# Two transformer blocks in f32: every operand tile is moved to a multiple of 256 bytes in SBUF

## The chip, the cores and the metric

The kernel runs on one core of one Trainium2 chip. The metric is the device time of one execution in microseconds, the median of several. Before the change it is 2309.09 us (three runs, 2305.04 to 2309.76).

## The reference

Two blocks follow each other on one sequence of 1024 tokens of width 1024, all in float32. Cut to what is computed:

```python
# first block
h = rms_norm(x, mix_norm_g);  proj = h @ w_in          # 1024 x 3080
fq, fk, fv, flog, dq, dk, dv = split(proj)
c = cumsum(log_sigmoid(flog + b_forget))               # 8 heads of 64, causal
fox = softmax(fq @ fk.T / 8 + c[t] - c[s]) @ fv
a = softmax(q1 @ k1.T / 8 + alibi) - lam * softmax(q2 @ k2.T / 8 + alibi)
diff = rms_norm(a @ dv) * 0.8                          # 4 heads, values of 128
x = x + concat(fox, diff) @ w_out
h = rms_norm(x);  x = x + (silu(h @ w_gate) * (h @ w_up)) @ w_down   # d_ff = 2816
x = rms_norm(x)
# second block
h = rmsnorm(x);  u, q, k, v = split(h @ w_in_2)        # 1024 x 2048
a = (mean of u over windows of 2, 4, 8, 16, less u) @ w_pool * pool_scale
b = neighbourhood attention of q, k, v on a 16 x 64 grid, with a bias
x = x + concat(a, b) @ w_out_2
h = rmsnorm(x);  x = x + square(relu(h @ w_up_2)) @ w_down_2         # d_ff = 4096
return rmsnorm(x)
```

## The kernel before

Tokens lie in tiles of 128 rows. Every factor of a large product is split into a high and a low half of type fp32r (`split`, L105 to L107: ScalarE copies the high half, VectorE or GpSimd subtracts it to get the low half), and a product is the sum of three matmuls (high by high, high by low, low by high), summed in PSUM in float32. Almost all of TensorE's work is such matmuls with a moving operand of 128 x 512 (7,756 of them) or about 128 x 256 (1,728 of 256 columns and 192 of 264), each with a stationary operand of 128 x 128. The lines are L155 (`proj_T`, queries and keys), L167 (`proj_tok`, values; the first weight piece has 2 x 4 x 264 columns because the forget gates are in it), L181 (`down`, output projection), L732 (`prod`, the first product of both feed-forward parts: gate and up in the first block, up in the second), L1204 (`ffn_deep`, the down products) and L1467 (`pool_mix`).

TensorE's order is written by hand: in the attention, pieces of projections are woven between the steps of the heads; in the feed-forward part the product of one unit follows the other. The instructions of the other engines are ordered by a scheduler from the program's order and the pools. Weights come by DMA from SyncE's queue into raw slots (`Weights.prefetch`, L52; two slots of 128 x 2112 float32, 8448 bytes per partition), and `get` (L67 to L80) splits them into `wh` and `wl` tiles of at least 128 x 1024, which go round a ring: two of each in pool `w1`, two of each in pool `w1b` (L355), then in `w1` alone. The other raw tiles (L667, L775, L1058) use the same slots.

SBUF is filled from two sides: pools on the left are laid from the lowest address up, pools with `side="right"` from the highest down, so a tile's address follows from the sizes of all the tiles before it on its side. In the kernel before, nearly every tile's size is a multiple of 256 bytes, but a few are not: `mhalf` and `lam` (4 bytes), the raw slots, the small `st` tiles, `wh` of 1056 columns, `lf`, the bias `b` of L491, and `psc`, `ws` and `edge` in `pool_mix`. The operand tiles come to lie as follows; each number is the start address modulo 256.

| operand | line | start modulo 256, moving / stationary | matmuls |
|---|---|---|---|
| gate, up and up products | L732 | 224 / 160 | 3192 |
| down products | L1204 | 224 / 224 | 2268 |
| projections, first block | L155 | 224 / 224 and 224 / 96 | 432 and 336 |
| projections, second block | L155 | 160 / 224 | 576 |
| output projections | L181 | 224 / 224, 224 / 160, 160 / 160 | 480, 240, 48 |
| pool mixer | L1467 | 192 / 0 | 24 |
| values, 256 columns | L167 | 224 / 160, 224 / 224, 96 / 224 | 960 in all |
| values, 264 columns | L167 | from 224 or 96 in steps of 32 / 224 | 192 |

A moving operand of 512 columns is 2048 bytes of a partition, one of 256 columns is 1024 bytes, a stationary one 512 bytes.

Of the kernel before, what the change touches and what calls it, by code (L numbers as in the profile page):

```python
# [9 lines left out]
F32 = mybir.dt.float32  # L10
F32R = mybir.dt.float32r
# [5 lines left out]
P = 128  # L17
NT = 8
# [18 lines left out]
class Weights:  # L37


    def __init__(self, k, raw_pool, depth):  # L40
        self.k, self.raw_pool, self.depth = k, raw_pool, depth
        self.todo, self.loaded = [], []
        self.pool_low = False
# [4 lines left out]
    def prefetch(self, depth=None):  # L48
        while self.todo and len(self.loaded) < (depth or self.depth):
            ap = self.todo.pop(0)  # L50
            n = ap.shape[-1]
            raw = self.raw_pool.tile([P, 2112], F32, tag="raw", name="raw")  # L52
            self.k.nc.sync.dma_start(raw[:, :n], ap)
            self.loaded.append((raw, n))

# [11 lines left out]
    def get(self):  # L67

        self.prefetch(1)
        raw, n = self.loaded.pop(0)  # L70
        out, m = [], n // 2
        for k in range(2):
            pool = self.slots.pop(0)
            self.slots.append(pool)
            h = pool.tile([P, max(m, 1024)], F32R, tag="wh", name="wh")
            l = pool.tile([P, max(m, 1024)], F32R, tag="wl", name="wl")
            self.k.split(h[:, :m], l[:, :m], raw[:, k * m:(k + 1) * m], self.pool_low)
            out.append((h[:, :m], l[:, :m]))
        self.prefetch()
        return out  # L80


class Kern:
    def __init__(self, tc, ctx, a):
        self.tc, self.nc, self.a = tc, tc.nc, a
        nc = self.nc
        self.const = ctx.enter_context(tc.tile_pool(name="const", bufs=1))
        self.raw = ctx.enter_context(tc.tile_pool(name="rawp", bufs=2))
        self.sm = ctx.enter_context(tc.tile_pool(name="small", bufs=8))
        self.ps = ctx.enter_context(tc.tile_pool(name="ps", bufs=4, space=PSUM))  # L90
        self.dram = ctx.enter_context(tc.tile_pool(name="scr", bufs=1, space=DRAM))
        self.ident = self.const.tile([P, P], F32, name="ident")
        make_identity(nc, self.ident)
        self.mhalf = self.const.tile([P, 1], F32, name="mhalf")
        nc.vector.memset(self.mhalf, -0.5)
        self.w = Weights(self, self.raw, 2)

# [234 lines left out]
    def block1_mix(self, enter_x):  # L332
        nc, tc, a = self.nc, self.tc, self.a
# [9 lines left out]
        at_ctx = tc.tile_pool(name="att", bufs=2)  # L343
        at = at_ctx.__enter__()
        cT = at.tile([P, NT, 8], F32, name="cT", bufs=1)
        lam = at.tile([P, 1], F32, name="lam", bufs=1)
        tri = at.tile([P, P], F32, name="tri", bufs=1)
        gd = at.tile([P, P], F32, name="gd", bufs=1)
        at2_ctx = tc.tile_pool(name="att2", bufs=2)
        with tc.tile_pool(name="act", bufs=1, side="right") as apool, \  # L350
                tc.tile_pool(name="w1", bufs=2, side="right") as wp, \
                tc.tile_pool(name="stage", bufs=2, side="right") as st:
            self.act_tiles(apool)
            with tc.tile_pool(name="w1b", bufs=2, side="right") as wpb:
                self.w.ring((wp, 2), (wpb, 2))  # L355
                self.w.depth, self.w.pool_low = 1, True
                norm, trans = self.norm_load(at, 0)
                self.w.pool_low = False
                for t in range(NT):
                    norm(t)  # L360
                    if t == 1:
                        w = self.w.get()
                self.w.depth, self.w.pool_low = 2, True
                lf = at.tile([P, NT, 8], F32, name="lf", bufs=1)
                for t in range(NT + LAG):
                    if t < NT:
                        trans(t)
                    if t == 5:
                        w1 = self.w.get()
                        self.w.pool_low = False  # L370
                    if t >= LAG:
                        self.proj_v(st, w, vd, 0, t - LAG, lf)
                nc.sync.dma_start(tri, a["tri"])
                nc.sync.dma_start(gd, a["gd"][0:1, :].partition_broadcast(P))
                nc.vector.tensor_scalar(gd, gd, 1.0 - LAM_INIT, None, ALU.mult)
                self.lambda_(at, lam)
                for t in range(NT):
                    self.proj_v(st, w1, vd, 1, t, lf)
                    if t == 1:
                        finish = self.forget(at, lf, cT, cd)  # L380
                    if t == 3:
                        w = self.w.get()
                for n in range(2):
                    for f, _ in self.proj_qk(st, qd, kd, n, w):
                        f()
                    w = None
                    if n == 0:
                        w = self.w.get()
                        finish()
            at2 = at2_ctx.__enter__()  # L390
            self.w.ring((wp, 2))
            fill, done = [], {("f", 0): 0, ("f", 1): 0}
            for kind, i in self.FILL:
                if (kind, i) == self.FILL[-1]:
                    fill.append((lambda: setattr(self.w, "depth", 1), 0.0))
                if kind == "v":
                    fill += self.proj_v_all(st, vd, i)
                else:
                    fill += self.proj_qk(st, qd, kd, i if kind == "f" else 4 + i)
                done[kind, i] = len(fill)  # L400
            fox = lambda i: self.fox_pair(at, at2, i, qd[i], kd[i], vd, cd, cT, tri, mxd[i], done["f", i])
            diff = lambda h: self.diff_head(at, at2, h, qd[4 + h], kd[4 + h], vd, gd, lam, mxd[4 + h], done["d", h])
            units = fox(0) + fox(1) + diff(0) + fox(2) + diff(1) + fox(3) + diff(2) + diff(3)
            steps = self.pipeline(units)
            cut = next(n for n, m in enumerate(steps) if m[2:] and m[2] == len(fill))
            self.weave(steps[:cut], fill, 0.0, -LEAD1)
# [74 lines left out]
    def forget(self, at, lfT, cT, cd):  # L481
# [3 lines left out]
        lf = mk("lf")  # L485
        for t in range(0, NT, 4):
# [1 line left out]
            for k in range(4):  # L488
                nc.tensor.transpose(pf[:8, k * P:(k + 1) * P], lfT[:, t + k, :], self.ident)
            nc.vector.tensor_copy(lf[:, t * P:(t + 4) * P], pf[:8, :])  # L490
        b = at.tile([8, 1], F32, tag="bf", name="bf", bufs=1)  # L491
        nc.sync.dma_start(b, a["b_forget"])
        z, u, t1, t2, t3 = mk("z"), mk("u"), mk("t1"), mk("t2"), mk("t3")
        nc.vector.tensor_scalar(z, lf, b, None, ALU.add)
# [170 lines left out]
        return units  # L665

    def mix_raw(self, mxd, c):  # L667
        m = self.raw.tile([P, 2112], F32, tag="raw", name="mixin")
        m = m[:, :2048].rearrange("p (k t) -> p k t", k=2)
        for kk in range(2):  # L670
            self.nc.sync.dma_start(m[:, kk, :], mxd[2 * c + kk])
        return m
# [100 lines left out]
        self.split(h[:, :, j * P:(j + 1) * P], l[:, :, j * P:(j + 1) * P], ps.rearrange("p (k t) -> p k t", t=P))  # L773

    def load_raw(self, src):  # L775
        t = self.raw.tile([P, 2112], F32, tag="raw", name="raw")[:, :src.shape[-1]]
        self.nc.sync.dma_start(t, src)
        return t

# [82 lines left out]
    def ffn(self, x, xd, mxd, wo, close_w, gi, n, gated, wts, wd, md, finish):  # L862


        nc, tc = self.nc, self.tc
# [3 lines left out]
        mixin = self.mix_raw(mxd, 3)  # L869
# [53 lines left out]
        for t in range(NT):  # L923
# [14 lines left out]
            k = t % 2  # L938
# [47 lines left out]
        wc = 4 * 512  # L986
# [10 lines left out]
        for i in range(G):  # L997
# [7 lines left out]
            b = self.one()  # L1005
# [49 lines left out]
                p2(i + L)  # L1055

            if i == G - 4:
                t = self.raw.tile([P, 2112], F32, tag="raw", name="raw")[:, :wc]  # L1058
                raws += [t, self.load_raw(wts[i + 2])]
                nc.sync.dma_start(t, wsrc(0, 2, wc))  # L1060
            elif i + 2 < G:
                raws.append(self.load_raw(wts[i + 2]))
# [338 lines left out]
    def pool_mix(self, at, st, mxd):  # L1401
# [3 lines left out]
        wh = at.tile([P, 512], F32R, name="wph", bufs=1)  # L1405
        wl = at.tile([P, 512], F32R, name="wpl", bufs=1)
        self.split(wh, wl, wf)
        psc = at.tile([P, 4], F32, name="psc", bufs=1)
        nc.sync.dma_start(psc, a["pscale"])
        rc = at.tile([P, 64], F32, name="rc", bufs=1)  # L1410
        nc.sync.dma_start(rc, a["rcount"].partition_broadcast(P))
# [18 lines left out]
        def sums(g, n):  # L1430

            u, gs, size = state[g]["u"], state[g], 2 << g
            if n == 0:
                gs["s"], gs["m"] = at.tile([P, 1040], F32, tag="ws", name="ws", bufs=1), 1039
                nc.vector.tensor_tensor(gs["s"][:, :1039], u[:, 0:1039], u[:, 1:1040], ALU.add)
                return
            s = gs["s"]
            if n <= g:
                step = 1 << n
                m = gs["m"] = gs["m"] - step  # L1440
                nc.vector.tensor_tensor(s[:, :m], s[:, 0:m], s[:, step:m + step], ALU.add)
                return
            off = 8 - size // 2
            edge = at.tile([P, 16], F32, tag="edge", name="edge")
            for k, t0 in ((0, 0), (1, S - 8)):
                ek, r_ = edge[:, k * 8:k * 8 + 8], rc[:, g * 16 + k * 8:g * 16 + k * 8 + 8]
                nc.vector.tensor_tensor(ek, s[:, off + t0:off + t0 + 8], r_, ALU.mult)
# [313 lines left out]
```

## Time and profile before

| | |
|---|---|
| median of three runs | 2309.09 us (2305.04 to 2309.76) |
| the profiled execution: its own time | 2302.17 us |
| its span, first to last instruction | 2300.5 us |
| TensorE (PE) busy | 2220.8 us, 97% |
| VectorE (DVE) busy | 1493.3 us, 65% |
| ScalarE (ACT) busy | 997.3 us, 43% |
| GpSimd (POOL) busy | 812.3 us, 35% |
| mean share of the DMA engines | 46.4% on SyncE's queue, 148 GB/s |
| granted TensorE clock, mean | 0.991 |

All rows come from the one profiled execution. A row of the timeline gives the start of a group of like instructions, the time from its first start to its last end, the engine, the line and the form, with x4 for four of them. The matmuls overlap in the record: one of 512 columns is shown as 390 ns long, but the next starts some 230 ns later. The time that a matmul costs in a stream is therefore the distance from one start to the next, here called the pitch. It is read by dividing the distance of two rows by the matmuls between them, or, within one row of n, by taking the recorded length of one (0.39 us) from the row and dividing by n - 1.

### The profile page before, as it was taken

The page shows a single profiled execution, that of the slowest core. Times are in us where ns is not written, and L with a number is a line of the kernel's source. Part 1 is how long each engine was busy: PE and PEld are TensorE (multiplying, and loading weights), DVE is VectorE, ACT ScalarE, POOL GpSimd, SP SyncE. Part 2 cuts the span into 40 slices and gives each one's busy share as a digit, 9 for nine tenths or more (in the row PEclk, how much of TensorE's full clock was granted, in tenths as well). Part 3 has the DMA queues.
Part 4 walks back from the last instruction along what each step waited for, and adds up shares of the span by engine and source line. Part 5 has one row for each costly group of instructions (what it writes and reads, how often), then busy time and mean ns, then how long its engine had stood idle before and what let it go on. Part 6 is the DMA issues. An engine that isn't in the chain of part 4 may idle for free.

```text
span 2300.5 us, 30691 instructions
## 1 busy us (share of the span) xinstructions
PE 2220.8 (97%) x11148; PEld 1870.5 (81%) x11148; DVE 1493.3 (65%) x2510; ACT 997.3 (43%) x1826; POOL 812.3 (35%) x742
## 2 busy tenths in 40 slices
PE   8999999989999999999999999999999999999998
PEld 8888898867788888878887888878778887878886
DVE  5356666677854545457889725687754444688888
ACT  5245555644433222223333536663454444434333
POOL 1055656563432323233235302110432222233335
PEclk9999999999999999999999999999999999999999
DMA  6487575651424333336311379884335444733202
GB/s 230 144 231 200 153 209 151 193 174 45 158 96 167 122 110 109 111 126 231 133 69 55 94 207 255 234 243 138 119 99 193 155 137 143 272 147 128 74 37 83
DMA packets 128615, 343.42 MB, mean 149 GB/s; under 512 B 12616, under 2 KB 49864, under 8 KB 113104
## 3 DMA queue, kind: packets, MB, share of 16 engines
q1 hardware_dynamic: 128320, 341.20, 46.4%
q8 instruction: 88, 1.44, 0.3%
q14 instruction: 63, 0.52, 0.1%
q10 hardware_dynamic: 144, 0.26, 0.0%
HBM read 254.35 MB, written 87.06 MB: 148 GB/s over the span
## 4 chain that ended last, share of the span: by engine, by line
PE 74%; DVE 13%; issue 4%; POOL 3%; ACT 3%; DMA 2%; SPq 0%; ACTq 0%; POOLq 0%; DVEq 0%
PE one L732 27%; PE one L1204 17%; PE one L155 12%; PE one L167 5%; PE one L181 4%; DVE o L107 4%; PE one L280 2%; PE one L571 1%; DVE x L187 1%; PE one L223 1%; DVE x L1209 1%; PE one L222 1%; PE one L633 1%; DVE wl L107 1%; DVE e L235 1%
## 5 line engine op out<-in xcount | busy, mean ns | idle before, releaser
L1204 PE MATMUL one<-o 128*128 128x512 f32 x2268 | 520.7, 391 | 11.8 <-DVE o L107 11.8
L1204 PEld LDWEIGHTS one<-o 128*128 128x128 f32 x2268 | 425.6, 188 | 105.9 <-DVE o L107 17.7
L732 PE MATMUL one<-o,wh 128*128 128x512 f32 x1216 | 309.9, 398 | 15.9 <-DVE u L1009 8.1
L107 DVE TENSOR_TENSOR wl<-raw,wh 128x512 fp32r<-128x512 f32 (+2 forms) x254 | 206.0, 825 | 143.8 <-ACT wh L106 141.0
L732 PEld LDWEIGHTS one<-o,wh 128*128 128x128 f32 x1216 | 230.3, 191 | 70.6 <-ACT o L106 7.0
L106 ACT ACTIVATE wh<-raw 128x512 fp32r<-128x512 f32 (+2 forms) x278 | 185.8, 699 | 86.4 <-POOL raw L721 53.1
L721 POOL TENSOR_TENSOR s<-raw 128x512 f32<-128x512 f32 x38 | 54.6, 1438 | 471.1 <-DMA raw<-in_wgu_dram 233.0
L732 PE MATMUL one<-o,wl 128*128 128x512 f32 x608 | 164.9, 393 | 0.0
L239 ACT ACTIVATE e<-e,st 128x768 f32<-128x768 f32 (+7 forms) x128 | 99.4, 776 | 134.1 <-DVE st L235 131.8
L1209 DVE TENSOR_TENSOR x<-x,one 128x512 f32<-128x512 f32 x184 | 121.9, 677 | 52.4 <-PE one L1204 52.3
L732 PEld LDWEIGHTS one<-o,wl 128*128 128x128 f32 x608 | 115.0, 189 | 24.9
L155 PE MATMUL one<-actH,wh 128*128 128x512 f32 x448 | 124.0, 398 | 0.2 <-DVE ptl L107 0.2
L155 PE MATMUL one<-actH,wl 128*128 128x512 f32 x448 | 123.6, 397 | 0.0
L155 PE MATMUL one<-actL,wh 128*128 128x512 f32 x448 | 123.6, 397 | 0.0
L1365 POOL TENSOR_SCALAR ne<-ne,st 128x384 f32<-128x384 f32 x64 | 39.5, 618 | 225.9 <-DVE st L241 207.5
L106 ACT ACTIVATE o<-tb 128x1024 fp32r<-128x1024 f32 (+1 forms) x42 | 42.8, 1031 | 165.4 <-DVE tb L721 165.3
L1029 DVE TENSOR_TENSOR u<-one,p 128x512 f32<-128x512 f32 x38 | 26.3, 691 | 135.5 <-PE one L732 135.4
L554 POOL TENSOR_SCALAR b<-negc,cT 128x640 f32<-128x640 f32 (+3 forms) x64 | 50.1, 784 | 153.5 <-DVE st L235 93.2
L721 POOL TENSOR_TENSOR raw<-raw 128x512 f32<-128x512 f32 x76 | 99.2, 1306 | 6.0
L834 ACT ACTIVATE f<-f 128x512 f32<-128x512 f32 x33 | 20.9, 632 | 181.0 <-DVE f L827 162.8
L187 DVE TENSOR_TENSOR x<-one,x 128x512 f32<-128x512 f32 x128 | 82.4, 681 | 25.8 <-PE one L181 25.4
L850 ACT ACTIVATE f<-f 128x512 f32<-128x512 f32 x48 | 30.4, 632 | 156.0 <-DVE f L827 131.3
(254 smaller groups left out, 4961.9 us busy)
## 6 DMA issues: line engine op xcount, KB each, us to landing
raw<-in_wgu_dram SPq DMA_DIRECT2D x22, 1024.0 KB, 5.2
raw<-in_wup_dram SPq DMA_DIRECT2D x16, 1024.0 KB, 5.3
mr<-f SPq DMA_DIRECT2D x64, 256.0 KB, 4.9
raw<-in_wdn_dram SPq DMA_DIRECT2D x14, 1024.0 KB, 5.0
wq<-in_wdn_dram SPq DMA_DIRECT2D x12, 1024.0 KB, 9.1
nbias<-in_nab_dram SPq DMA_DIRECT2D x32, 384.0 KB, 4.9
mq<-mr SPq DMA_DIRECT2D x12, 1024.0 KB, 6.3
raw<-in_wgu_dram SPq DMA_DIRECT2D x22, 512.0 KB, 4.0
```

The source lines that it names most:

```text
L106: self.nc.scalar.activation(h, src, AF.Copy)
L107: (self.nc.gpsimd if pool else self.nc.vector).tensor_tensor(l, src, f32(h), ALU.subtract)
L155: self.nc.tensor.matmul(ps, lhsT=w_[:, k, cols:cols + P], rhs=ac[:, 4 * j + k, half * 512:half * 512 + 512], start=(n == 0), stop=(n == 23))
L167: self.nc.tensor.matmul(ps, lhsT=ac[:, 4 * j + k, t * P:(t + 1) * P], rhs=w_[:, k, :], start=(n == 0), stop=(n == 23))
L181: nc.tensor.matmul(dst[h], lhsT=a_[:, kk, t * P:(t + 1) * P], rhs=w_[:, h * 512:(h + 1) * 512], start=(n < 2), stop=(n >= last))
L187: nc.vector.tensor_tensor(xs, p_, xs, ALU.add)
L239: nc.scalar.activation(e, e, AF.Exp, bias=mx, scale=-1.0, accum_out=sm)
L554: nc.gpsimd.tensor_scalar(b[:, :nk], nc_row[:, :nk], cT[:, qt, h:h + 1], 1.0, ALU.add, ALU.mult)
L721: (self.nc.gpsimd if pool else self.nc.vector).tensor_tensor(out, a, b, ALU.subtract)
L732: self.nc.tensor.matmul(ps, lhsT=l, rhs=r, start=(first and n == 0), stop=(n == total - 1), skip_group_check=True)
L1204: nc.tensor.matmul(ps, lhsT=l[:, sl], rhs=r[:, sb], start=(start and n == 0), stop=(n == total - 1), skip_group_check=True)
L1209: nc.vector.tensor_tensor(dst, dst, ps, op)
```

## The change

The first tiles on each side are pads (`padl`, `padr`), so that what follows begins at a multiple of 256 bytes; the sizes that were no such multiple are rounded up, or the tile is made a part of another. The raw slots shrink from 8448 to 8192 bytes. The first weight piece, with 2112 columns, no longer fits a raw slot and gets a tile of its own in a new pool `w1c`; the split weights of the first pieces go round eight slots over three pools in place of four over two.

```diff
@@ Weights.prefetch
-            raw = self.raw_pool.tile([P, 2112], F32, tag="raw", name="raw")
+            if n > 2048:
+                raw = self.wider.tile([P, n], F32, name="raw", bufs=1)
+            else:
+                raw = self.raw_pool.tile([P, 2048], F32, tag="raw", name="raw")
@@ Weights.get
-            h = pool.tile([P, max(m, 1024)], F32R, tag="wh", name="wh")
-            l = pool.tile([P, max(m, 1024)], F32R, tag="wl", name="wl")
+            h = pool.tile([P, max(-(-m // 64) * 64, 1024)], F32R, tag="wh", name="wh")
+            l = pool.tile([P, max(-(-m // 64) * 64, 1024)], F32R, tag="wl", name="wl")
@@ Kern.__init__
         self.const = ctx.enter_context(tc.tile_pool(name="const", bufs=1))
+        self.const.tile([P, 32], F32, name="padl")
+        padr = ctx.enter_context(tc.tile_pool(name="padr", bufs=1, side="right"))
+        padr.tile([P, 56], F32, name="padr")
...
-        self.mhalf = self.const.tile([P, 1], F32, name="mhalf")
+        self.cols = self.const.tile([P, 64], F32, name="cols")
+        self.mhalf, self.lam = self.cols[:, 0:1], self.cols[:, 1:2]
@@ block1_mix
-        lam = at.tile([P, 1], F32, name="lam", bufs=1)
+        lam = self.lam
...
-            with tc.tile_pool(name="w1b", bufs=2, side="right") as wpb:
-                self.w.ring((wp, 2), (wpb, 2))
+            with tc.tile_pool(name="w1b", bufs=2, side="right") as wpb, \
+                    tc.tile_pool(name="w1c", bufs=2, side="right", reuse_waits="tile") as wpc:
+                self.w.wider = wpc
+                self.w.slots = [wpc, wpc, wp, wp, wpc, wpc, wpb, wpb]
...
-                lf = at.tile([P, NT, 8], F32, name="lf", bufs=1)
+                lf = at.tile([P, P], F32, tag="dt2", name="lf", bufs=4)[:, :64].rearrange("p (t h) -> p t h", h=8)
@@ forget
-        b = at.tile([8, 1], F32, tag="bf", name="bf", bufs=1)
+        b = at.tile([8, 64], F32, tag="bf", name="bf", bufs=1)[:, :1]
@@ mix_raw, load_raw, ffn: raw tiles
-        m = self.raw.tile([P, 2112], F32, tag="raw", name="mixin")
+        m = self.raw.tile([P, 2048], F32, tag="raw", name="mixin")
...
@@ pool_mix
-        psc = at.tile([P, 4], F32, name="psc", bufs=1)
+        psc = at.tile([P, 64], F32, name="psc", bufs=1)[:, :4]
...
-                gs["s"], gs["m"] = at.tile([P, 1040], F32, tag="ws", name="ws", bufs=1), 1039
+                gs["s"], gs["m"] = at.tile([P, 1088], F32, tag="ws", name="ws", bufs=1), 1039
...
-            edge = at.tile([P, 16], F32, tag="edge", name="edge")
+            edge = at.tile([P, 24], F32, tag="edge", name="edge")[:, :16]
```

With the change, all 7,756 matmuls of 512 columns and all 1,728 of 256 have both operands at 0 modulo 256. The 192 matmuls of 264 columns have the stationary operand at 0 and the moving one at 0, 32, 64 or 96, because their columns still follow each other in steps of 1056 bytes.

TensorE's and GpSimd's instructions keep their order. On the other three engines the order differs in the first 95 us alone. ScalarE, while the activations are normed and transposed (`actH` is an evacuated transposition, `vt` a finished value tile, `raw_405` and `raw_407` the third and fourth weight pieces), before:

```order
L106 ACTIVATE vt_378<-one_353 128x2x2x64
L106 ACTIVATE actH_123<-one_390 128x4x128
L106 ACTIVATE actH_123<-one_439 128x4x128
L106 ACTIVATE vt_434<-one_409 128x2x2x64
L106 ACTIVATE actH_123<-one_446 128x4x128
L476 ACTIVATE st_595<-st_593 128x1
L476 ACTIVATE st_599<-st_597 128x1
L106 ACTIVATE vt_478<-one_453 128x2x2x64
L106 ACTIVATE actH_123<-one_483 128x4x128
L106 ACTIVATE actH_123<-one_490 128x4x128
```

and after (the same third and fourth pieces are now `raw_412` and `raw_414`):

```order
L114 ACTIVATE vt_385<-one_360 128x2x2x64
L114 ACTIVATE actH_127<-one_397 128x4x128
L114 ACTIVATE wh_1012<-raw_414 128x1024
L114 ACTIVATE vt_441<-one_416 128x2x2x64
L114 ACTIVATE actH_127<-one_446 128x4x128
L114 ACTIVATE actH_127<-one_453 128x4x128
L114 ACTIVATE wh_1016<-raw_414 128x1024
L114 ACTIVATE vt_485<-one_460 128x2x2x64
L114 ACTIVATE actH_127<-one_490 128x4x128
L114 ACTIVATE actH_127<-one_497 128x4x128
```

The two copies of the fourth piece, which stood behind the values of the second weight piece, now stand among the transpositions; VectorE's two subtractions move with them. With a free slot earlier, the next loads move up too. SyncE's queue, where values go out to DRAM (`vd`) and weights come in, before:

```order
L432 DMA vd0_86<-vt_434 128x512
L432 DMA vd0_86<-vt_478 128x512
L432 DMA vd0_86<-vt_522 128x512
L432 DMA vd0_86<-vt_552 128x512
L432 DMA vd0_86<-vt_582 128x512
L53 DMA raw_763<-in_wv_dram 128x2048
L432 DMA vd1_87<-vt_628 128x512
```

and after:

```order
L443 DMA vd0_91<-vt_441 128x512
L443 DMA vd0_91<-vt_485 128x512
L56 DMA raw_770<-in_wv_dram 128x2048
L443 DMA vd0_91<-vt_529 128x512
L443 DMA vd0_91<-vt_559 128x512
L443 DMA vd0_91<-vt_589 128x512
L56 DMA raw_1020<-in_wqk_dram 128x2048
L443 DMA vd1_92<-vt_635 128x512
```

The load of the fifth piece has passed three stores of values, and the load of the sixth, which stood behind the stores of `vd1`, has passed those.

## Rows read from the trace of the kernel before

**Rows 1.** The page: busy time by engine, and the costliest group of instructions
```profile
PE 2220.8 (97%) x11148; PEld 1870.5 (81%) x11148; DVE 1493.3 (65%) x2510; ACT 997.3 (43%) x1826; POOL 812.3 (35%) x742
...
L1204 PE MATMUL one<-o 128*128 128x512 f32 x2268 | 520.7, 391 | 11.8 <-DVE o L107 11.8
```

**Rows 2.** Chain of waits, its longest pieces: start us, us, what
```profile
662.75 340.90 PE one L732 x1488
...
1699.78 225.51 PE one L732 x984
```

**Rows 3.** Stages: length, busy us of PE, PEld, DVE, ACT, POOL, clock, DMA share, GB/s
```profile
130.00:480.00 350.00, 343.44 (x2131) 304.35 (x2129) 238.50 (x684) 202.71 (x472) 214.22 (x275) 1.00 0.67 191
...
640.00:1010.00 370.00, 368.73 (x1620) 302.12 (x1619) 184.83 (x275) 109.54 (x198) 111.33 (x79) 1.00 0.36 120
...
1300.00:1380.00 80.00, 79.53 (x481) 70.46 (x482) 22.77 (x36) 25.89 (x43) 0.74 (x2) 1.00 0.65 178
1380.00:1560.00 180.00, 175.99 (x983) 152.82 (x982) 127.29 (x349) 114.07 (x260) 37.13 (x62) 0.99 0.86 238
...
2030.00:2270.00 240.00, 238.10 (x1047) 195.65 (x1046) 208.02 (x196) 89.72 (x92) 85.91 (x32) 1.00 0.23 89
```

**Rows 4.** Timeline of PE, down products L1204: start us, us, engine, line, form
```profile
1188.74 12.63 PE L1204 MATMUL one<-o 128*128 128x512 f32 x55
```

**Rows 5.** Timeline of PE, projections L155, first block, then second block
```profile
107.60 1.07 PE L155 MATMUL one<-actH,wh 128*128 128x512 f32 x4
...
112.13 1.07 PE L155 MATMUL one<-actH,wl 128*128 128x512 f32 x4
...
1334.29 1.09 PE L155 MATMUL one<-actL,wh 128*128 128x512 f32 x4
...
1348.29 1.09 PE L155 MATMUL one<-actL,wh 128*128 128x512 f32 x4
```

**Rows 6.** Timeline of PE, values L167, 264 columns, then 256
```profile
24.43 0.64 PE L167 MATMUL one<-wl,actH 128*128 128x264 f32 x4
24.91 0.64 PE L167 MATMUL one<-wh,actL 128*128 128x264 f32 x4
...
26.36 0.65 PE L167 MATMUL one<-wh,actL 128*128 128x264 f32 x4
...
113.51 0.64 PE L167 MATMUL one<-wl,actH 128*128 128x256 f32 x4
...
115.43 0.64 PE L167 MATMUL one<-wh,actL 128*128 128x256 f32 x4
...
1325.35 0.63 PE L167 MATMUL one<-wl,actH 128*128 128x256 f32 x4
...
1331.94 0.63 PE L167 MATMUL one<-wh,actH 128*128 128x256 f32 x4
```

**Rows 7.** Timeline of PE, values L167 behind a wait for a DMA
```profile
126.69 1.05 PE L167 MATMUL one<-wh,actH 128*128 128x256 f32 x4
...
129.24 1.02 PE L167 MATMUL one<-wh,actH 128*128 128x256 f32 x4
```

**Rows 8.** Timeline of PE, transpositions of 128 columns, L135 and L280
```profile
23.83 0.27 PE L135 MATMUL one<-ident,y 128*128 128x128 f32 x1
...
132.32 1.36 PE L280 MATMUL one<-ident,e 128*128 128x128 f32 x11
```

**Rows 9.** Timeline of PE, pool mixer L1467
```profile
1500.17 0.39 PE L1467 MATMUL one<-pmh,wph 128*128 128x512 f32 x1
...
1501.33 0.39 PE L1467 MATMUL one<-pmh,wpl 128*128 128x512 f32 x1
```

**Rows 10.** Timeline of ACT and of DVE, weight splits, the idle time before in brackets
```profile
35.06 0.39 ACT L106 ACTIVATE vt<-one 128x256 fp32r<-128x256 f32 x1 [3.08 <-DMA vd<-vt]
...
89.73 1.06 ACT L106 ACTIVATE wh<-raw 128x1024 fp32r<-128x1024 f32 x1 [1.72 <-PE one L155]
...
88.04 1.23 DVE L107 TENSOR_TENSOR wl<-raw,wh 128x1024 fp32r<-128x1024 f32 x1 [1.61 <-ACT wh L106]
```

More of the change, by code (lines that the diff above doesn't have):

```diff
@@ L667, in mix_raw @@
     def mix_raw(self, mxd, c):
-        m = self.raw.tile([P, 2112], F32, tag="raw", name="mixin")
-        m = m[:, :2048].rearrange("p (k t) -> p k t", k=2)
+        m = self.raw.tile([P, 2048], F32, tag="raw", name="mixin")
+        m = m.rearrange("p (k t) -> p k t", k=2)
         for kk in range(2):
@@ L775, in load_raw @@
     def load_raw(self, src):
-        t = self.raw.tile([P, 2112], F32, tag="raw", name="raw")[:, :src.shape[-1]]
+        t = self.raw.tile([P, 2048], F32, tag="raw", name="raw")[:, :src.shape[-1]]
         self.nc.sync.dma_start(t, src)
@@ L1057, in ffn @@
             if i == G - 4:
-                t = self.raw.tile([P, 2112], F32, tag="raw", name="raw")[:, :wc]
+                t = self.raw.tile([P, 2048], F32, tag="raw", name="raw")[:, :wc]
                 raws += [t, self.load_raw(wts[i + 2])]
```

## The prediction, made before the changed kernel had run

> **What bounds the kernel.** I read the busy times first. TensorE is busy for 2220.8 of 2300.5 us, 97%; VectorE, next, for 65% [rows 1]. Then the chain of waits: its longest pieces are runs of TensorE alone, 1488 matmuls of L732 that fill 340.90 us without a break, then 984 in 225.51 us [rows 2]. The stages say the same: between 640 and 1010 us TensorE is busy for 368.73 of 370 us and VectorE for 184.83; between 1300 and 1380 us 79.53 of 80 against 22.77 [rows 3]. The granted clock there is 1.00, the higher of the two levels, 2.4 GHz [rows 3]. So the end is set by how long TensorE takes per matmul, and by little else.
>
> The question then is what one matmul costs in such a stream, and that is read from distances between starts. 512 columns at 2.4 GHz are 213.3 ns. In the stream of L732 the pitch is 340.90 / 1488 = 229.1 ns [rows 2]; in L1204 it is (12.63 - 0.39) / 54 = 226.7 ns [rows 4]; L155 takes (112.13 - 107.60) / 20 = 226.5 ns in the first block and (1348.29 - 1334.29) / 60 = 233.3 ns in the second [rows 5]; L1467 takes 1.16 / 5 = 232 ns [rows 9]. These are the same instruction on the same shapes, all in the full clock, and they go by the addresses in the table of the section on the kernel: 229.1 at 224/160, 226.6 at 224/224, 233.3 at 160/224, 232 at 192/0 (moving / stationary, modulo 256). So 13 to 20 ns in each matmul are not columns, and their size depends on where the operands lie. No matmul of 512 columns in this kernel has its moving operand at 0.
>
> Two rows tell what kind of time it is. Behind a wait for a DMA the clock falls to its lower level, and there 12 matmuls of 256 columns take 2.55 us, 212.5 ns each [rows 7], which is 256 columns at 1.2 GHz with nothing on top; at the higher level 256 columns take 117.7 or 120.0 ns [rows 6], 11 to 13 ns over their 106.7. Time that vanishes when the array is slow is time in which the array is not fed. And the transpositions, 128 columns in (1.36 - 0.27) / 10 = 109 ns [rows 8], twice the 53.3 ns of 128 columns and 2.3 more, read only half as many bytes per ns, and show hardly any of it.
>
> **What feeds it, as I read the rows.** Count the stretches of 256 bytes that a moving operand touches. One of 512 columns (2048 bytes) from 224, 192 or 160 touches nine, one from 0 would touch eight; one of 256 columns touches five, or four from 0. A stretch is 64 columns, 26.7 ns. The pitches of the best pair, 226.6 for nine and 120.0 for five, differ by 106.6, four times 26.7: both are stretches x 26.7 less 13. And 264 columns, eight more, also touch five from every address that they have (224, 0, 32 and so on): they take (26.36 - 24.43) / 16 = 120.6 ns, against 120.0 for 256, where eight columns alone would be 3.3 ns [rows 6]; the first four, with 0 among their addresses, take 0.48 us, as four of the sixteen do on average. By this reading eight stretches would be fed in 200 ns, less than the 213.3 of the columns, and the array would be the bound again.
>
> **The change part by part.** (1) All matmuls of 512 and 256 columns get both operands at 0. No row has that pair, so the pitch that follows is bounded: from below by 213.3 ns, the columns, from above by 233.3, the dearest pair of the trace [rows 5]. I take the columns and the 2.3 ns that the transpositions keep, the nearest row of a matmul that is fed in time: 215.6 ns for 512 columns, 109 for 256. Then, with the counts of the table:
>
> - L732: 3192 x (229.1 - 215.6) = 43.1 us.
> - L1204: 2268 x (226.7 - 215.6) = 25.2 us.
> - L155, second block: 576 x (233.3 - 215.6) = 10.2 us; first block: 768 x 10.9 = 8.4 us, all at the pitch of the rows shown.
> - L181, priced like L1204: 768 x 11.1 = 8.5 us. L1467: 24 x 16.4 = 0.4 us.
> - L167: 960 of 256 columns x 9.5 (117.7 and 120.0 less 109) = 9.1 us; its 192 of 264 columns still touch five stretches: nothing.
>
> That is 105 us of TensorE's time. What of it reaches the end? All of L732 and of L155's second block, 53.3 us, since nothing else is near its limit there [rows 3]. Of L1204 I take half, 12.6: in the second block's stretch VectorE is busy for 208.02 us to TensorE's 238.10 [rows 3], TensorE already waits 11.8 us for its splits [rows 1], and with 11 ns less in each of 1047 matmuls, 11.6 us, VectorE's 208 stand against 226.5, 92% in place of 87%. Of L155's first block, L181, L167 and L1467, 26.4 us together, also half, 13.2: they are woven between attention steps, where VectorE (238.50 of 350 us), POOL (214.22) and the DMA engines (a share of 0.67, 0.86 in the second block) carry much [rows 3]; what TensorE saves there comes back in part as a wait for them. The sum is 79.1 us.
>
> (2) The splits of the fourth weight piece move up among the transpositions: two ScalarE copies of 1.06 us and two VectorE subtractions of 1.23 us [rows 10]. I cost this at nothing: ScalarE waits there, 3.08 us in one place for a DMA [rows 10]. If that cover is gone, it is 2 x 1.06 + 2 x 1.23 = 4.6 us. It gains nothing either, because the places that they leave were not waited for: ScalarE itself waited 1.72 us for TensorE just before such a copy [rows 10].
>
> (3) SyncE's queue: two weight loads pass stores of values. A load of 1 MB at the 191 GB/s of the stretch from 130 us [rows 3] takes 5.5 us, by which the stores behind it are late; they are read back only in the attention. Nothing, at most 5.5 us if the first head waits.
>
> (4) The pads, rounded sizes and merged tiles issue nothing. VectorE's and ScalarE's operands move with the rest; these engines idle 35% and 57% [rows 1], so a small change of theirs stays hidden outside the down products.
>
> The profiled execution took 2302.17 us, so it would be 2223; the median of the runs stands 6.9 us higher, 2309.09, and gives 2230 us.
>
> The Trainium skill bears on the value in (1). Its page "TensorE: Matmul & The Clock Gate", section "Wait — 56ns, not 53.3ns?", gives the start-to-start distance as the columns over the clock when cold, and about 2.5 ns more when warm. The cold half agrees with the 212.5 ns here; the warm half does not, for 226.6 to 233.3 ns stand where it says 215.8. By it, as an estimate, what is aligned would save 0.2 ns less in each matmul of 512 columns, 1.5 us in all, than with my value.
>
> **Rivals.**
>
> *The 13 ns stay* (an issue cost of each matmul at this rate; only the differences between pairs go). For it: L1204, with equal offsets, is the cheapest of all, and every matmul of 512 columns shows at least 13 ns [rows 4, 5]. Against it: they are gone at the lower clock and in the transpositions [rows 7, 8]. Every pair comes to 226.7: L732 3192 x 2.4 = 7.7, L155's second block 576 x 6.6 = 3.8, the 240 of L181 at L732's pair 0.6: 12 us, 2297.
>
> *Addresses at multiples of 32 are as good as any*: the differences are those of the stages (what the other engines and DMAs read and write at the time). For it: each pair of addresses belongs to a stage of its own. Against it: L155 in the two blocks differs by 6.8 ns in streams of TensorE alone, with no break in either [rows 5]. Then nothing moves: 2309. The Trainium skill speaks for this one: "SBUF — State Buffer", section "Specifications (TRN2)", puts cachelines at 16 bytes, and every operand here starts on one already. No run here shows such a line.
>
> *Slower: moving and stationary operand collide.* When both start at 0, the weight load of the next matmul and the stream of this one walk through the same places in step, and the feed stalls. Place: every matmul of 512 columns; price: the 233.3 ns of the dearest pair. For it: the pair with the stationary operand at 0 takes 232 ns [rows 9]. Against it: 224/224 is in step too, and cheapest. L732 3192 x 4.2 = 13.4, L1204 2268 x 6.6 = 15.0, L155 432 x 6.8 = 2.9, L181 480 x 6.6 = 3.2: 34.5 us more, 2344. It decides from a mean pitch above about 229 ns.
>
> **How the numbers follow.** Chances: forecast 0.50, the 13 ns stay 0.23, addresses don't matter 0.13, collision 0.14. The forecast's own range is 2204 (all 105 us reach the end) to 2257 (6.7 ns, the distance between the pitches 226.6 and 233.3, stay on each: L732 29.0, L155's second block 7.7, half of 30.6 for the rest, 52 us in all). To hold 8 of 10 the range has to take in the next two, with their noise and a cost of (2): 2200 to 2313; the collision is left out. About 0.2%, 4.6 us, is what a measurement can tell here. Faster by more: the forecast (0.49) and most of the first rival (0.21), 0.70; the same: 0.15; slower: 0.15.
>
> **What would show it.** In the profile after: the pitch of L732 in its long run near 216 ns, 1488 of them in 321 us and not 341; L1204 at the same pitch but with more waits for VectorE's `o`; L155 of both blocks alike; 256 columns near 109 and 264 still near 120. If L732 stands at 226.7, the first rival is right; at 229, the second; above, the third. The forecast is wrong too if the pitch falls and the stages don't, because the waits for VectorE, POOL or a DMA grow by as much.

## The result, and the profile after

The changed kernel takes 2294.35 us (four runs, 2291.3 to 2298.97) against 2308.95 before: a ratio of 0.9949, with a 95% interval of 0.9931 to 0.9967. It is faster, by 8 to 16 us, and not by the 79 that were forecast. The time is that of the first rival (2297): the 13 ns on each matmul stayed, and only the differences between pairs of addresses went. It lies inside the stated range, 2200 to 2313, only because that range was drawn to hold the first two rivals as well; the forecast's own range ended at 2257. The time before is now the median of four runs.

The busy times hardly moved; this row answers to [rows 1], for the profiled execution of 2298.97 us, the slowest of the four:

```profile
PE 2214.2 (96%) x11148; PEld 1874.8 (82%) x11148; DVE 1489.0 (65%) x2510; ACT 996.8 (43%) x1826; POOL 810.0 (35%) x742
```

The longest piece of the chain of waits (start, us, what) answers to [rows 2]; line 743 is the former 732, 1215 the former 1204, 163 the former 155 and 175 the former 167:

```profile
662.79 337.59 PE one L743 x1488
```

337.59 / 1488 = 226.9 ns, where 229.1 stood and 215.6 were forecast. The other lines of 512 columns come to the same number where TensorE streams them alone. The timeline of TensorE, in the order of [rows 4, 5, 6] (start, us, engine, line, form):

```profile
1184.62 14.67 PE L1215 MATMUL one<-o 128*128 128x512 f32 x64
...
103.70 1.07 PE L163 MATMUL one<-actH,wl 128*128 128x512 f32 x4
...
111.86 1.07 PE L163 MATMUL one<-actH,wl 128*128 128x512 f32 x4
...
1332.64 1.07 PE L163 MATMUL one<-actL,wh 128*128 128x512 f32 x4
...
1341.71 1.07 PE L163 MATMUL one<-actH,wl 128*128 128x512 f32 x4
...
24.63 0.65 PE L175 MATMUL one<-wl,actH 128*128 128x264 f32 x4
...
26.56 0.65 PE L175 MATMUL one<-wh,actL 128*128 128x264 f32 x4
...
1320.19 0.64 PE L175 MATMUL one<-wh,actH 128*128 128x256 f32 x4
...
1331.23 0.64 PE L175 MATMUL one<-wh,actL 128*128 128x256 f32 x4
```

Down products: (14.67 - 0.39) / 63 = 226.7 ns, unchanged. L163: 8.16 / 36 = 226.7 in the first block (226.5 before, at 224/224) and 9.07 / 40 = 226.8 in the second, where 233.3 stood. The 264 columns keep 120.6 ns. The 256 columns of the second block got dearer: 11.04 / 92 = 120.0 ns for 117.7, so being aligned is not the cheapest place for them.

In the profiled pair the execution falls by 3.2 us alone (2302.17 to 2298.97). TensorE's order is the same in both, so the starts of each of its matmuls can be set side by side. The changed kernel gains 0.20 us in every 20 us of L732, 3.5 us by 1031 us, and 1.8 us from 1330 to 1530 us, where the projections of the second block stand; and it gives back 1.3 to 1.5 us at a time at a few places, at 1033 and at 2026 us of the kernel before, for instance. At these two the granted clock fell in this execution and not in the other. Two windows, of the kernel before and of the changed one (columns as in [rows 3], the clock third from the end):

```profile
1030.00:1050.00 20.00, 17.87 (x78) 14.72 (x79) 12.38 (x18) 7.42 (x11) 5.20 (x4) 1.00 0.56 186
...
2000.00:2030.00 30.00, 28.34 (x124) 22.77 (x123) 29.68 (x24) 8.34 (x9) 19.98 (x6) 1.00 0.40 161
```

```profile
1030.00:1050.00 20.00, 20.00 (x86) 16.46 (x85) 12.21 (x17) 8.41 (x12) 5.18 (x4) 0.96 0.57 187
...
2000.00:2030.00 30.00, 28.16 (x117) 22.81 (x116) 29.20 (x24) 12.08 (x12) 14.40 (x5) 0.94 0.27 97
```

Both executions wait there (3.5 us for `u` near 1040), and whether the clock falls behind such a wait differs from one execution to the next: the four timed ones of the changed kernel ran at a mean clock of 0.991 (2291.3 us), 0.992 (2292.3), 0.990 (2296.4) and 0.988 (2299.0). One profile is therefore no measure of an effect of this size; the pitches are, because they repeat to 0.2 ns.

### The profile page after: what moved, and what is told of

Its sections match the earlier page's. It is cut to its first block, busy times and chain, and to the rows that moved or that the text cites. A ratio compares the mean times of both kernels' runs of the same rounds, so it can differ in the third digit from the quotient of the medians.

```text
span 2297.2 us, 30687 instructions
## 1 busy us (share of the span) xinstructions
PE 2214.2 (96%) x11148; PEld 1874.8 (82%) x11148; DVE 1489.0 (65%) x2510; ACT 996.8 (43%) x1826; POOL 810.0 (35%) x742
## 4 chain that ended last, share of the span: by engine, by line
PE 70%; DVE 13%; issue 6%; POOL 4%; ACT 3%; DMA 2%; SPq 0%; ACTq 0%; POOLq 0%; DVEq 0%
PE one L743 26%; PE one L1215 17%; PE one L163 11%; PE one L175 5%; DVE o L115 4%; PE one L189 3%; DVE x L195 1%; PE one L288 1%; PE one L582 1%; DVE e L243 1%; DVE x L1220 1%; PE one L231 1%; PE one L230 1%; ACT e L247 1%; PE one L1396 1%
## 5 line engine op out<-in xcount | busy, mean ns | idle before, releaser
L732 POOL TENSOR_TENSOR s<-raw 128x512 f32<-128x512 f32 x38 | 53.9, 1418 | 467.7 <-DMA raw<-in_wgu_dram 206.6
L163 PE MATMUL one<-actH,wh 128*128 128x512 f32 x448 | 122.8, 396 | 0.2 <-DVE ptl L115 0.2
L163 PE MATMUL one<-actL,wh 128*128 128x512 f32 x448 | 122.8, 396 | 0.0
L163 PE MATMUL one<-actH,wl 128*128 128x512 f32 x448 | 122.4, 395 | 0.0
L732 POOL TENSOR_TENSOR raw<-raw 128x512 f32<-128x512 f32 x76 | 98.3, 1294 | 6.0
```

Source lines behind the costliest of these rows:

```text
L163: self.nc.tensor.matmul(ps, lhsT=w_[:, k, cols:cols + P], rhs=ac[:, 4 * j + k, half * 512:half * 512 + 512], start=(n == 0), stop=(n == 23))
L732: (self.nc.gpsimd if pool else self.nc.vector).tensor_tensor(out, a, b, ALU.subtract)
```

## The experiments

Two theories stood after the result. A: a matmul's cost depends on the distance between the starts of its moving and its stationary operand, and equal starts are the cheapest for 512 columns, wherever they are. B: a multiple of 256 bytes matters as such. C, the third, puts the gain to the other parts of the change (slots, earlier splits).

**Streams of matmuls by themselves (bench1).** The operands are two tiles of fp32r, or of bf16, the starts are shifted, and nothing else runs:

```diff
+    for mo, so in PAIRS:       # starts of moving and stationary operand, bytes modulo 256
+        stream(f"f512m{mo}s{so}", m, w, mo // 4, so // 4, 512)      # 48 matmuls, no wait between
+    for n in (512, 384, 256, 128):
+        stream(f"b{n}m0s0", mb, wb, 0, 0, n)                        # the same in bf16
```

> A kernel of streams of 48 matmuls each, with no wait between them, that computes nothing of the reference: each stream has one pair of start addresses (moving / stationary, modulo 256), one width and one type. Theory A (what counts is the distance between the two starts; equal starts are cheapest anywhere): 512 columns of fp32r at 0/0, 32/32, 64/64, 128/128 and 224/224 all take 226.7 ns, 224/160 takes 229, 160/224 takes 233, and the pairs with a stationary start of 32 to 224 lie between 227 and 236. Theory B (a start at a multiple of 256 counts): only 0/0 takes 226.7 or less, 32/32 to 128/128 take 229 or more. Theory C (addresses don't count, the stages did it): all pairs take the same within 0.5 ns. On the 13.3 ns over the columns: if they are a cost of feeding 4-byte operands, bf16 takes 216 ns for 512 columns at 0/0; if every matmul pays them, bf16 takes 226.7 as well.

The timeline of the streams; a name tells type, columns and the moving start (the stationary start, a number at the end of the name, isn't printed). The pitch is the distance to the next stream's start over 48:

```profile
22.21 11.08 PE L44 MATMUL f512m32s<-m,w 128*128 128x512 f32 x48
33.12 11.07 PE L44 MATMUL f512m64s<-m,w 128*128 128x512 f32 x48
44.03 11.09 PE L44 MATMUL f512m128s<-m,w 128*128 128x512 f32 x48
...
76.87 11.36 PE L44 MATMUL f512m160s<-m,w 128*128 128x512 f32 x48
88.07 11.35 PE L44 MATMUL f512m192s<-m,w 128*128 128x512 f32 x48
...
199.85 11.16 PE L44 MATMUL f512m64s<-m,w 128*128 128x512 f32 x48
210.85 11.32 PE L44 MATMUL f512m128s<-m,w 128*128 128x512 f32 x48
...
334.24 10.52 PE L44 MATMUL b512m224s<-mb,wb 128*128 128x512 bf16 x48
344.60 10.52 PE L44 MATMUL b512m160s<-mb,wb 128*128 128x512 bf16 x48
```

32/32 and 64/64 take 10.91 / 48 = 227.3 ns, 128/128 227.5. 160/224 takes 11.20 / 48 = 233.3, as in the kernel; so does 192/0. 64/0 takes 11.00 / 48 = 229.2, the value of 224/160, which has the same distance. All 19 pairs go by the distance alone, within about 1 ns: 227 at 0, 229 at 64 (moving less stationary, modulo 256), 232 to 234 at the others tried. Theory A holds and B falls; addresses do count, and whether the slots add something is left to the next run. And bf16 takes 10.36 / 48 = 215.8 ns from all four pairs tried, 0/0, 32/0, 224/160 and 160/224: here the address counts for fp32r and not for bf16, and the 13 ns stand on fp32r alone.

**Every operand at 32 (eq32), and the old places with the new slots (mixed).** Only the pads change. Mixed brings back the old places of the products and of the second block; in the first block the 336 projections that stood at 224/96, and the values that stood at 96/224, now have equal starts, 224/224:

```diff
-        self.const.tile([P, 32], F32, name="padl")
+        self.const.tile([P, 40], F32, name="padl")        # eq32; mixed: 72
-        padr.tile([P, 56], F32, name="padr")
+        padr.tile([P, 112], F32, name="padr")             # eq32; mixed: 64
```

> The changed kernel with larger pads, so that every operand starts 32 bytes behind a multiple of 256, moving and stationary alike (32/32). Theory A: like the changed kernel, 2294 us within 5, the long run of the gate and up products at 226.9 ns per matmul. Theory B: no better than before, 2309 or more, and that run at 229 or more.

> The changed kernel with all its slots and sizes, but pads that put the left side at 160 and the right side at 224, as they lay before: gate and up products 224/160, projections of the second block 160/224, down products 224/224. Theories A and B: like the kernel before, 2309 us within 5, with 229.1, 233.3 and 226.7 ns per matmul. Theory C (the gain came from the slots, the earlier splits or the smaller raw tiles): like the changed kernel, 2294, while the pitches may stay as before.

Measured: eq32 2297.14 us, ratio to before 0.996 (0.9947 to 0.9973); mixed 2305.23 us, ratio 1.000 (0.9989 to 1.0012). The chain's longest piece, of eq32 and of mixed:

```profile
660.56 337.59 PE one L743 x1488
```

```profile
663.79 340.88 PE one L743 x1488
```

32/32 gives the changed kernel's 226.9 ns to the hundredth of a microsecond, and 224/160 gives the 229.1 of before with all the other edits in place. Theory A again; the slots, the earlier splits and the smaller raw tiles are worth nothing that shows in the time.

**One side at 64 (left64).** A dose the other way: the left pad grows by 64 bytes, so the gate and up products stand at 0/64.

```diff
-        self.const.tile([P, 32], F32, name="padl")
+        self.const.tile([P, 48], F32, name="padl")
```

> The changed kernel with the left pad 64 bytes larger: the left side starts at 64, the right side at 0. Theory A (the distance between the two starts decides, with the prices of the streams measured by themselves): gate and up products at 0/64 take 233.3 instead of 226.7, 3192 x 6.6 = 21 us; 240 of the output projections 1.6 us; projections of the second block at 64/0 take 228.9, 576 x 2.1 = 1.2 us; 384 matmuls of 256 columns at 0/64 fall from 120.0 to 113.3, -2.6 us: 21 us more than the changed kernel, about 2316, some 7 us slower than before. Rival (a start at 0 of the moving operand is what matters, the stationary one counts little): gate and up products stay at 226.7 to 229, and the time between 2294 and 2302.

Measured: 2312.73 us, ratio to before 1.0034 (1.0021 to 1.0047), 7.1 us slower by the medians where some 7 were expected. That agreement is closer than its parts: the distances from start to start of like matmuls, in the two profiles side by side, add up to 12 us more, and the two spans differ by 11.0 us. Why the medians differ by less is open. The moving operand of these products lies at 0 all the same, so its own place is not what counts:

```profile
660.73 347.48 PE one L743 x1488
```

347.48 / 1488 = 233.5 ns. Two parts of the expectation failed. The projections of the second block stand at 64/0, for which the streams gave 229.2 ns and 228.9 was expected; they took (1364.81 - 1342.41) / 96 = 233.3 ns, no less than before at 160/224:

```profile
1342.41 1.10 PE L163 MATMUL one<-actL,wh 128*128 128x512 f32 x4
...
1364.81 1.10 PE L163 MATMUL one<-actL,wh 128*128 128x512 f32 x4
```

And the 256 columns of the second block that stand at 0/64 took 113 ns in a few groups and 118 in most, where 113.3 was expected for all. So the distance modulo 256 decides in the streams and in most lines of the kernel, but it is not the whole of it; what else counts is open.

**The value weights at 192 (vshift).** An attempt to be better than the change: 576 of the 256-column matmuls are given the distance that took 113.3 ns in a stream.

```diff
-            h = pool.tile([P, max(-(-m // 64) * 64, 1024)], F32R, tag="wh", name="wh")
-            l = pool.tile([P, max(-(-m // 64) * 64, 1024)], F32R, tag="wl", name="wl")
+            e = max(-(-m // 64) * 64, 1024)
+            hl = pool.tile([P, 2 * e + self.extra], F32R, tag="wh", name="wh")
+            h, l = hl[:, off:off + m], hl[:, off + e:off + e + m]       # off = 48 for value pieces
...
```

> The changed kernel, with the weights of the value pieces (256 columns, first block, 576 matmuls) begun 192 bytes behind a multiple of 256, so that moving / stationary is 192/0, the distance that took 113.3 ns in the streams; all else stays at 0/0. The high and the low half of a weight piece share one tile for this. Theory A: these matmuls fall from 120.0 to 113.3 ns, 576 x 6.7 = 3.8 us, of which half lies woven between attention steps: 2 to 4 us less than the changed kernel, about 2291. Rival (256 columns at 0/0 are as good, the 113.3 belongs to the empty chip of the streams): 120 stays, no difference.

Measured: 2294.84 us, ratio to before 0.9958 (0.9943 to 0.9973). That cannot be told from the changed kernel. The timeline shows the pitch that was expected, in some places:

```profile
60.17 1.07 PE L176 MATMUL one<-wh,actH 128*128 128x256 f32 x8
61.08 0.62 PE L176 MATMUL one<-wh,actL 128*128 128x256 f32 x4
...
65.16 0.62 PE L176 MATMUL one<-wh,actL 128*128 128x256 f32 x4
65.61 1.07 PE L176 MATMUL one<-wh,actH 128*128 128x256 f32 x8
```

From 60.17 to 65.61 are 48 matmuls in 5.44 us, 113.3 ns, in this stretch. Over the first block as a whole about half of the distances are 113 or 114 ns and half 117 to 119, as in left64 without a reason that shows; the median is 117, where the changed kernel has 120. The 2 to 4 us are not seen in the time; a new wait of 1.0 us for the splits, which now share a tile, takes part of them. Whether the rest is lost or only hidden in the spread is open.

**What the 13 ns are (bench2, bench3).** More streams: finer distances, fewer stationary columns, other widths, the same places read again (the first two lines are of bench2, the others of bench3).

```diff
+    for cols in (96, 64, 32):
+        stream(f"f512c{cols}x", m, w, 0, 0, 512, cols)          # 128 x cols stationary
+    stream("samem", m, w, 0, 0, 512, mstep=0)                   # the same moving columns each time
+    stream("again8x", m, w, 0, 0, 512, again=8)                 # 64 columns, eight times in one matmul
```

> Streams of 48 matmuls again, nothing of the reference computed: the moving operand at 0, the stationary one at finer distances, other widths, and with only 96, 64 or 32 stationary columns. Theory L (the excess is the next weight load, which reads SBUF beside the stream; where the two starts lie to each other decides how much of it collides): with fewer stationary columns the 13.3 ns of 0/0 shrink, to about 7 with 64 columns and about 4 with 32. Rival F (each fp32r matmul pays a fixed 13.3 ns): 226.7 ns with any number of stationary columns. For 256 columns both expect the cheapest start of the stationary operand at 64 (113.3 ns) and 120 at 0. Starts that differ by 4, 8 or 16 bytes: like 0 (226.7) if places are counted in lines of 32 bytes or more, otherwise higher.

> Streams of 48 fp32r matmuls again, nothing of the reference computed, most with only 32 stationary columns, so that the weight load is short, and with widths from 64 to 512. Theory P (what stays at equal starts belongs to the moving operand's own stream: 6.7 ns for each begun 1024 bytes of it): 64 to 256 columns take the columns and 6.7 ns, 260 to 512 the columns and 13.3 ns or a little more, from any start. Theory S (my reading before: the count of 256-byte stretches that the moving operand touches): 256 columns from 4, 16, 32, 64 or 128 take 20 ns more than from 0, since five stretches stand in place of four. Theory W (the weight load's reading causes it all): 32 columns leave 2.5 ns. If it is the reading of different places that costs, the streams that read the same columns again (again8x: 64 columns eight times) fall to 216 ns; if it is the type, they stay at 226.7. bf16 stays 2.5 ns over its columns at every width.

bench2, 512 columns with 128, 96, 64 and 32 stationary columns, then 256 with 128 at 0/0 and at 0/64, then 64 and 32 at 0/0, and 128 columns:

```profile
21.20 11.05 PE L39 MATMUL f512s0x<-m,w 128*128 128x512 f32 x48
32.09 11.32 PE L39 MATMUL f512s4x<-m,w 128*128 128x512 f32 x48
...
98.47 11.21 PE L39 MATMUL f512c96x<-m,w 128*96 128x512 f32 x48
109.51 11.20 PE L39 MATMUL f512c64x<-m,w 128*64 128x512 f32 x48
120.55 11.28 PE L39 MATMUL f512c32x<-m,w 128*32 128x512 f32 x48
131.67 11.13 PE L39 MATMUL f512d96x<-m,w 128*96 128x512 f32 x48
...
164.93 5.91 PE L39 MATMUL f256s0x<-m,w 128*128 128x256 f32 x48
170.68 5.85 PE L39 MATMUL f256s16x<-m,w 128*128 128x256 f32 x48
...
187.69 5.61 PE L39 MATMUL f256s64x<-m,w 128*128 128x256 f32 x48
193.14 5.86 PE L39 MATMUL f256s80x<-m,w 128*128 128x256 f32 x48
...
238.49 5.60 PE L39 MATMUL f256c64x<-m,w 128*64 128x256 f32 x48
243.93 5.61 PE L39 MATMUL f256c32x<-m,w 128*32 128x256 f32 x48
...
370.86 5.52 PE L39 MATMUL f128s128x<-m,w 128*128 128x128 f32 x48
```

For 512 columns 10.89 / 48 = 226.9 ns with 128 stationary columns, 230.0 with 96 and 64, 231.7 with 32: fewer stationary columns do not lower it. Theory L falls for them, and a fixed 13.3 (rival F) does not fit the rise either. For 256 columns it does go down, from 119.8 to 113.3 ns with 64 columns; 0/64 with all 128 reaches the same 113.5.

bench3:

```profile
22.56 3.05 PE L42 MATMUL n128c32x<-m,w 128*32 128x128 f32 x48
25.44 4.41 PE L42 MATMUL n192c32x<-m,w 128*32 128x192 f32 x48
29.68 5.62 PE L42 MATMUL n256c32x<-m,w 128*32 128x256 f32 x48
35.14 7.04 PE L42 MATMUL n320c32x<-m,w 128*32 128x320 f32 x48
42.02 8.48 PE L42 MATMUL n384c32x<-m,w 128*32 128x384 f32 x48
...
150.41 6.01 PE L42 MATMUL n256c32m4x<-m,w 128*32 128x256 f32 x48
156.25 5.60 PE L42 MATMUL n256c32m16x<-m,w 128*32 128x256 f32 x48
161.69 5.79 PE L42 MATMUL n256c32m32x<-m,w 128*32 128x256 f32 x48
167.32 5.76 PE L42 MATMUL n256c32m64x<-m,w 128*32 128x256 f32 x48
172.92 5.61 PE L42 MATMUL n256c32m128x<-m,w 128*32 128x256 f32 x48
178.37 11.04 PE L42 MATMUL samew<-m,w 128*128 128x512 f32 x48
189.25 11.04 PE L42 MATMUL samem<-m,w 128*128 128x512 f32 x48
...
211.01 11.04 PE L42 MATMUL again8x<-m,w 128*128 128x512 f32 x48
221.89 11.04 PE L42 MATMUL again2x<-m,w 128*128 128x512 f32 x48
```

256 columns from 0 take 5.46 / 48 = 113.8 ns, from 4 121.7, from 16 113.3, from 32 117.3, from 64 116.7, from 128 113.5: five stretches of 256 bytes in place of four cost 0 to 8 ns, not 20, so my count of stretches (theory S) falls. The same weights, the same columns, and even 64 columns read eight times over all take 10.88 / 48 = 226.7 ns. So the 13 ns are not the reading of so many different places; with bf16's 215.8 beside it they belong to fp32r. Theory W falls with the 113.8 (2.5 over the columns was 109.2), and theory P in its steps: 320 columns take 143 ns, 10 more than the columns, not 13, and 512 with 32 stationary columns 231.6, 18 more.

## Why the prediction was wrong, point by point

- *What bounds the kernel*: right. L732's long run keeps its pitch without a break in every version, and the time went the way of that pitch: down with 226.9 ns, back up with 229.1 (mixed), further up with 233.5 (left64).
- *Part (1), the value of the aligned pair*: the step that failed. I took 215.6 ns, the columns and the 2.3 ns of the transpositions; it is 226.7. Of the 13.5 ns per matmul of L732, 2.2 came: (340.90 - 337.59) / 1488, or 7.1 us in 3192 and not 43.1. L1204's term, 25.2 us, is nothing. L155's second block gave 1.9 us and not 10.2: 6.4 ns in each of the some 200 distances up to 1380 us, and 2 ns in the some 310 that are woven between attention steps. The distances from start to start of like matmuls, in the two profiles side by side, add up to 9 us of the 105: L732 6.6, L155 2.9, L181 0.8, and the values of the second block take 0.7 back.
- *L155's first block* was priced at the pitch of the rows shown, 226.5 ns, for all 768. That row is of the 224/224; the 336 at 224/96 took 233 ns where they stand by themselves, before 100 us. It gave 1.0 us, where half of 8.4 was forecast.
- *Why that value seemed near*: two readings. The count of stretches rested on 264 columns costing what 256 cost, and on 226.6 and 120.0 differing by four stretches. Both numbers were right and the count of stretches was not their cause: 256 columns can be had for 113.3 ns, and 120.0 was one distance of several. And the transpositions were no row of a matmul that is fed in time. In the streams, 128 columns of fp32r take (5.52 - 0.27) / 47 = 111.7 ns with 128 stationary columns and 2.88 / 48 = 60.0 with 32 (bf16 takes 55.8): the pace of so short a matmul goes by its stationary operand. The transpositions' 109 ns are near the 111.7 and are put down to the same; no run varied the transpositions themselves.
- *What spoke for the rival and was weighed too lightly*: no matmul of 512 columns showed less than 13 ns, and the pair with equal starts was the cheapest. I put 0.23 on it. "Gone at the lower clock" was right as read, but it fits both: a feed that is some 6% slower than the fast array would be fast enough for the slow one. That is argued, not tested.
- *The first rival's own sum*: 7.7 + 3.8 + 0.6 = 12 us, against 9 by the distances side by side and 8 to 16 by the time. It took all of L155's second block at the pitch of its undisturbed part, missed the 336 of the first block, and missed the 256 columns of the second block, 384 x 2.3 = 0.9 us the other way.
- *Second rival*: wrong, as mixed and left64 show. With it the cacheline of 16 bytes from the Trainium skill ("SBUF — State Buffer", "Specifications (TRN2)") tells nothing here, for starts 32 and 64 bytes apart differ by 2 to 7 ns. *Collision*: wrong in place, since equal starts are the cheapest, but right that the places of the two operands count together: 0/64 costs the 233.3 ns it named.
- *The 2.5 ns of the Trainium skill* ("TensorE: Matmul & The Clock Gate", "Wait — 56ns, not 53.3ns?"): the trace of the kernel disagreed, and the streams agree in bf16 alone, with 215.8 ns; fp32r shows 13.3 ns or more in its place at 512 columns.
- *Parts (2) to (4)*: right as far as the traces show. At 121 us the changed kernel stood 0.22 us ahead of the one before, with the splits and the loads moved, and its wait for the first head's operands was no longer than before, 3.2 us against 3.3. At 127 us it stood 0.9 us behind: its granted clock in that stretch was at the lower level (a mean of 0.50 of full from 124 to 127 us, against 0.95). Half of L1204's gain, kept back for VectorE, was never put to the test.

## What to carry to other kernels

Where TensorE streams fp32r, read the pitch against columns over clock for every line, and compare lines by where their operands start before explaining the rest. For a value that no row has, the row to take is one that shares the mechanism: width, type, and what paces it; a short stream on its own settles in one run what the kernel's rows can only suggest. Two kernels that differ by 0.5% are told apart by their pitches and by repeated runs, and not by the spans of one profile each.

## What the runs showed of the hardware that was not expected

- An fp32r matmul of 512 columns by 128 takes 226.7 ns at best in all these streams, 13.3 over its columns; bf16 takes 215.8 from all four pairs of addresses tried. 226.7 is 17/16 of 213.3, and the 113.3 of 256 columns is 17/16 of 106.7, but 384 columns took 173.2 at best, where 17/16 would be 170.0; what causes the excess is open.
- On top come, with 128 stationary columns, 0 to 7.5 ns that depend on the distance between the two starts modulo 256. One line of left64 did not follow it (233.3 ns at 64/0). The best distance for 512 columns (0) is among the worst for 256 (120.0; best 113.3 with the stationary operand 64 behind). Four bytes are enough, and one way only: 0/4 took 232.4 ns in bench2, 0/252 took 226.7.
